# Pool mixer and second norm of a decoder layer: whole float32 products, a small bias, transposes, another opening

## The chip, the cores and the metric

The kernel runs on one core of a Trainium2 chip. The metric is the device time of one execution in microseconds (us). The engines are TensorE (PE in the profile: matrix products into the accumulation memory PSUM), VectorE (DVE), ScalarE (ACT), GpSimd (POOL) and SyncE (SP, which here issues all transfers). Each engine works through its own list of instructions in order; semaphores make one engine wait for another.

## The reference

One layer: a norm, a causal pooling mixer, a residual sum, a second norm, a gated network with a short convolution, a residual sum. `D_MODEL` and `SEQ` are 1024, the hidden width is 2816.

```python
def rms_norm(x, g):
    y = x * lax.rsqrt(jnp.mean(x * x, axis=-1, keepdims=True) + EPS)
    return y * g

def pool_mixer(x, w, b, scale):            # windows 2, 4, 8, 16: one per group of 256 columns
    cs = cumulative sum of x over the sequence
    window_sum = cs[pos + 1] - cs[max(pos + 1 - w_len, 0)]
    d = window_sum / count - x             # per group
    return scale * (einsum('bsgc,gcd->bsgd', d, w) + b)

def conv_ffn(x, w_in, conv_w, conv_b, w_out):
    h = causal_depthwise_conv(x @ w_in, conv_w, conv_b)
    val, gate = jnp.split(h, 2, axis=-1)
    return (jax.nn.silu(gate) * val) @ w_out

x = x + pool_mixer(rms_norm(x, norm_mix_g), ...)
x = x + conv_ffn(rms_norm(x, norm_ffn_g), ...)
```

## The kernel before

**Precision.** TensorE takes two kinds of float32 here. Plain float32 is exact enough as it is. The rounded kind (`fp32r`) runs faster but keeps fewer bits. So the large products are split: `hi` is the operand rounded by ScalarE, `lo` the rest that VectorE subtracts, and a product is the sum of hi x hi, hi x lo and lo x hi: three passes.

**The mixer, per tile of 128 rows** (`j` from 0 to 7):

- `stat(j)` calls `rstd_of` (L127): ScalarE squares the tile and sums (L130), takes a root (L131), and five small VectorE steps (L132 to L137) give the reciprocal root with one correcting step.
- `mixer_norm(j)` (L145) scales a constant band matrix by that number per row: `bandr`. The band holds 1/w inside the window, and 1/w - 1 on the diagonal.
- `mixer_window(j)` (L188): eight plain products (L151) of the tile with the band give window mean minus tile, transposed, in the PSUM tile `psd`. The first 16 positions are mended: by a factor for tile 0 (L196), by `edges` for the others (L198). ScalarE writes `dh` (L199), VectorE the rest `dl` (L200).
- `mixer_out(j)` (L206): 24 products (L214) of the parts with the weights' parts `wph`, `wpl`, and two (L215) that add the bias, into `psy`. VectorE adds the tile (L217), which is stored for the last residual sum (L218); then the second norm's statistics (`st_b`) and a diagonal matrix `diag` of the reciprocal roots (L221).
- `ffn_operand(j)` (L233): eight plain products (L237) of the tile with `diag` turn and norm it at once into `pst`. The gain of the second norm is one number per partition there: seven pieces on ScalarE (L242), the eighth on VectorE (L244), into `n2f`. Then sums and differences (L271) and splits (L259, L260) make the network's operands.

`edge_norm` and `mixer_edges` do the same for the last 16 rows of every tile (`x_edge`), which reach into the next tile. `mixer_weights` scales the pool weights (L178) and splits them (L183, L184). `mixer_bias` forms scale x bias in all 128 partitions, the high part in 64 of them, the low part in the other 64 (L157 to L162), from a broadcast load of 512 KB.

**The network.** Its first product runs as seven products of half blocks per block of hidden columns instead of eight (operands named `B11`, `T1`, `B22`, `T2` and so on; L303). `load_in(n)` loads 1 MB of weights into a `raw` buffer, `prep_in` makes sums and splits. The first operands (`A11`, `A12` of blocks 0 and 1) and three such products are woven into the last rounds of the mixer loop (L389 to L413); everything from L415 is the network proper.

**Buffers and order.** A tile asks for one of `bufs` buffers under a tag and waits until the last reader of the buffer's former tile is done. Three tags matter: `raw` has two buffers of 8 KB per partition (`wp_raw`, `rows_b`, then the network's blocks), `ha` has one (`x_edge`, later the network's `ha`), `ps` has three in PSUM (`psd`, `psy`, `pst`, `ps_edges`). Each engine's list is laid down when the kernel is built, by a planner that follows the program's order where operands are ready; `tc.issue_after(ins)` puts what is written inside behind `ins` in the list of that instruction's engine, without waiting for its end.

Of the kernel before, what the change touches and what calls it, by code (L numbers as in the profile page):

```python
# [7 lines left out]
F32 = mybir.dt.float32  # L8
# [18 lines left out]

CW, CB, GM = 0, 3 * 2 * NF, 4 * 2 * NF
# [5 lines left out]
BD = B0 + NG * P  # L34

NOPS_A = 3
ACT_GAIN = 7
# [6 lines left out]
def trunk_kernel(ctx: ExitStack, tc: tile.TileContext, x, consts, par, rows, pool_w, w_in, w_out, out):  # L44
# [31 lines left out]
    def load_x(j):  # L76
        if j < 2 or j == NS - 1:
            xs[j] = work.tile([P, D], F32, tag="hl", name=f"x{j}", bufs=7)
        else:
            xs[j] = pp.tile([P, D], F32, tag="x", name=f"x{j}", bufs=5)  # L80
        nc.sync.dma_start(xs[j], x[j * P : (j + 1) * P, :])
# [8 lines left out]
    nc.gpsimd.memset(x_edge[:HALO, :], 0.0)  # L90
    for g, w in enumerate(WINDOWS):

        e = edge_band[:, g, :].rearrange("p (j t) -> p j t", t=HALO)
        nc.gpsimd.memset(edge_band[:, g, :], 1.0 / w)
        affine(e, e, ALU.is_gt, 0.0, w - HALO, [[-HALO, NS], [-1, HALO]], 1)
        affine(e, e, ALU.is_ge, 0.0, HALO - 1, [[HALO, NS], [0, HALO]], -1)
    for g, w in enumerate(WINDOWS):

        m = band[:, g, :]
        nc.gpsimd.memset(m, 1.0 / w)  # L100
        affine(m, m, ALU.is_ge, 0.0, 0, [[1, P]], -1)
        affine(m, m, ALU.is_gt, 0.0, w, [[-1, P]], 1)
        affine(m, m, ALU.not_equal, 1.0 / w - 1.0, 0, [[1, P]], -1)
    par_sb = const.tile([P, NPAR], F32, tag="par", name="par_sb")
    wp_raw = raw_tile("wp_raw").rearrange("p a (c d) -> p (a c) d", d=GRP)
    rows_b = raw_tile("rows_b")
    scale_b, bias_b = rows_b[:, 0, :], rows_b[:, 1, :]
    load_x(0)
    nc.sync.dma_start(cst, consts)
    nc.sync.dma_start(x_edge[HALO:, :], x.rearrange("(j r) d -> j r d", r=P)[: NS - 1, P - HALO :, :])  # L110
# [11 lines left out]
    nc.vector.memset(eps_t, EPS)  # L122
    ident = cst[:, :FAC]
    fac = cst[:, FAC:B0].rearrange("p (c t) -> p c t", t=HALO)
    band0 = cst[:, B0:].rearrange("p (g s) -> p g s", s=P)

    def rstd_of(src, name):  # L127
# [3 lines left out]
        nc.scalar.activation(st[:, 1:2], st[:, 0:1], AF.Sqrt, bias=eps_t, scale=1.0 / D)  # L131
        nc.vector.tensor_scalar(st[:, 0:1], st[:, 0:1], 1.0 / D, EPS, op0=ALU.mult, op1=ALU.add)  # L132
        nc.vector.reciprocal(st[:, 2:3], st[:, 1:2])

        nc.vector.scalar_tensor_tensor(st[:, 3:4], st[:, 2:3], st[:, 0:1], st[:, 2:3], op0=ALU.mult, op1=ALU.mult)
        nc.vector.tensor_scalar(st[:, 3:4], st[:, 3:4], -0.5, 1.5, op0=ALU.mult, op1=ALU.add)
        nc.vector.tensor_tensor(st[:, 2:3], st[:, 2:3], st[:, 3:4], ALU.mult)  # L137
        return st[:, 2:3]

    bands, marks, stats = {}, {}, {}  # L140

    def edge_norm():
        nc.vector.tensor_scalar(edge_band, edge_band, rstd_of(x_edge, "e"), None, op0=ALU.mult)

    def mixer_norm(j):  # L145
        t = bands[j] = pp.tile([P, NG, P], F32, tag="bandr", name=f"bandr{j}", bufs=2)
        nc.vector.tensor_scalar(t, band if j else band0, stats[j], None, op0=ALU.mult)

    def windows(ps, src, weights):
        for c in range(NK):  # L150
            nc.tensor.matmul(ps[:, c * P : (c + 1) * P], src[:, c * P : (c + 1) * P], weights[:, c // 2, :], start=True, stop=True)  # L151


    bias_hl = pp.tile([P, D], F32R, tag="bias_hl", name="bias_hl")
    mean_w = pp.tile([P, P], F32R, tag="mean_w", name="mean_w")

    def mixer_bias():  # L157
        nc.vector.memset(mean_w.bitcast(F32), 2.0 / P)
        nc.vector.tensor_tensor(bias_b, bias_b, scale_b, ALU.mult)
# [489 lines left out]
```

## Time and profile before

| | us |
|---|---|
| median of 3 runs (721.27 to 721.67) | 721.29 |
| the profiled execution | 723.45 |
| its span, first to last instruction | 721.7 |
| TensorE busy in the span | 698.9 (97%) |
| VectorE busy | 609.7 (84%) |
| ScalarE busy | 352.3 (49%) |
| the network's products, L303 (1848) and L576 (924), mean ns of one | 390 to 394 |

How to read it: a line of the table by stretch has the length, then for PE, PEld (weight loads), DVE, ACT and POOL the busy time and the number of instructions, then the clock granted to TensorE as a share of full speed, the busy share of the transfer engines, and GB/s. A line of the chain of waits has start, length, engine, tile and line of the work that the end of the span hung on. A line of the groups has line, engine, operation, output and inputs, shapes and count, then busy time and the mean of one in ns, then idle time of the engine ahead of it and what ended that. A matrix product's recorded length overlaps the next one's, so what a row of them costs is told by the distance between starts, or by the chain. One call of a plain float32 product leaves two records.

### The profile page before, as it was taken

To read this page: it belongs to the slowest core of one execution; us is meant where nothing else is said; L and a number is where in the kernel's file an instruction comes from. 1 tells how busy PE (TensorE), PEld (TensorE's weight loads), DVE (VectorE), ACT (ScalarE), POOL (GpSimd) and SP (SyncE) were. 2 spreads that over 40 slices of the span, in tenths; PEclk is the share of its full clock that TensorE was granted. 3 is DMA by queue.
4 is the path that set the end of the run, shared out by engine and by line. 5 is a ranking of instruction groups with operands and counts; after the bars stand their busy time and mean duration, and the time that the engine had idled before them with its cause. 6 is when DMAs were issued, how large, how long until landed. Compare 5 with 4: busy or idle time off the path is not lost.

```text
span 721.7 us, 8803 instructions
## 1 busy us (share of the span) xinstructions
PE 698.9 (97%) x3252; PEld 580.2 (80%) x3252; DVE 609.7 (84%) x941; ACT 352.3 (49%) x566; POOL 7.7 (1%) x33
## 2 busy tenths in 40 slices
PE   3799999999999999999999999999999999999997
PEld 3799977888888888888888888888888788888886
DVE  3788999999888898888888888877996998798994
ACT  4597746554444444444444444444553444344441
POOL 4000000000000000000000000000000000000000
PEclk9899999999999999999999999999999999999999
DMA  9722030222222222222122112227999910005241
GB/s 266 282 89 84 34 117 0 118 88 88 88 87 88 88 88 89 87 88 81 66 89 73 58 75 87 88 89 264 315 321 312 308 54 1 0 1 190 87 152 67
DMA packets 30881, 83.83 MB, mean 116 GB/s; under 512 B 3335, under 2 KB 4487, under 8 KB 28023
## 3 DMA queue, kind: packets, MB, share of 16 engines
q1 hardware_dynamic: 30839, 83.28, 32.8%
q8 instruction: 25, 0.41, 0.2%
q14 instruction: 17, 0.14, 0.1%
HBM read 63.34 MB, written 19.92 MB: 115 GB/s over the span
## 4 chain that ended last, share of the span: by engine, by line
PE 80%; DVE 11%; DMA 6%; issue 1%; SPq 1%; ACT 1%; DVEq 0%; ACTq 0%
PE Y L303 23%; PE oP L576 21%; PE X L303 15%; PE Z L303 15%; PE psy L214 3%; DMA blk<-g_dram 3%; PE psd L151 2%; DMA x<-in_x_dram 1%; PE pst L237 1%; DVE n2f L271 1%; DVE oBP L70 1%; DVE T L260 1%; DMA blk<-in_w_out_dram 1%; DVE blk L271 1%; DVE oAP L70 1%
## 5 line engine op out<-in xcount | busy, mean ns | idle before, releaser
L576 PE MATMUL oP<-oBP,oAP 128*128 128x512 f32 x924 | 210.8, 390 | 1.0 <-ACT oBP L69 0.6
L576 PEld LDWEIGHTS oP<-oBP,oAP 128*128 128x128 f32 x924 | 173.2, 188 | 38.5 <-DVE oBP L70 1.4
L303 PE MATMUL X<-B,A11s 128*128 128x512 f32 x264 | 65.6, 394 | 0.7 <-DVE A11s L70 0.7
L303 PE MATMUL Y<-T,S2s 128*128 128x512 f32 x264 | 65.1, 394 | 1.1 <-DVE T L260 1.0
L303 PE MATMUL Z<-B,S4s 128*128 128x512 f32 x264 | 64.1, 392 | 0.6 <-DVE r L337 0.6
L303 PE MATMUL Z<-T,S1s 128*128 128x512 f32 x264 | 64.6, 393 | 0.0
L303 PE MATMUL Y<-T,S3s 128*128 128x512 f32 x264 | 64.3, 392 | 0.0
L303 PE MATMUL Y<-T,A22s 128*128 128x512 f32 x264 | 64.1, 392 | 0.0
L303 PE MATMUL X<-B,A12s 128*128 128x512 f32 x264 | 63.4, 390 | 0.0
L303 PEld LDWEIGHTS Y<-T,S2s 128*128 128x128 f32 x264 | 49.2, 188 | 13.2 <-DVE T L260 1.5
L303 PEld LDWEIGHTS X<-B,A11s 128*128 128x128 f32 x264 | 49.3, 188 | 12.3 <-DVE A11s L70 1.1
L303 PEld LDWEIGHTS Z<-B,S4s 128*128 128x128 f32 x264 | 49.5, 188 | 11.8 <-issue 1.1
L303 PEld LDWEIGHTS Z<-T,S1s 128*128 128x128 f32 x264 | 49.5, 188 | 11.4 <-ACT S1s L69 0.2
L303 PEld LDWEIGHTS Y<-T,S3s 128*128 128x128 f32 x264 | 49.6, 188 | 11.2
L303 PEld LDWEIGHTS Y<-T,A22s 128*128 128x128 f32 x264 | 49.5, 188 | 11.1 <-ACT val L350 0.3
L303 PEld LDWEIGHTS X<-B,A12s 128*128 128x128 f32 x264 | 49.5, 188 | 10.3
L361 ACT ACTIVATE gate<-gate 128x1024 f32<-128x1024 f32 x22 | 23.4, 1061 | 43.5 <-DVE gate L352 43.5
L69 ACT ACTIVATE oBP<-blk 128x512 fp32r<-128x512 f32 x32 | 20.2, 633 | 46.9 <-PE oP L576 41.6
L351 DVE SCALAR_TENSOR_TENSOR val<-ha,par_sb,val 128x1023 f32<-128x1023 f32 x22 | 28.2, 1282 | 12.5 <-ACT val L350 12.5
L343 DVE TENSOR_TENSOR ha<-Z,q 128x512 f32<-128x512 f32 x20 | 13.8, 691 | 23.9 <-PE Z L303 23.9
L69 ACT ACTIVATE S4s<-win 128x512 fp32r<-128x512 f32 x22 | 13.9, 633 | 40.4 <-PE Z L303 35.9
L350 ACT ACTIVATE gate<-hb,par_sb 128x1024 f32<-128x1024 f32 x22 | 27.4, 1245 | 11.9 <-DVE hb L345 11.9
(130 smaller groups left out, 1094.2 us busy)
## 6 DMA issues: line engine op xcount, KB each, us to landing
win<-in_w_in_dram SPq DMA_DIRECT2D x22, 1024.0 KB, 4.8
g_dram<-val SPq DMA_DIRECT2D x22, 512.0 KB, 2.6
blk<-g_dram SPq DMA_DIRECT2D x33, 256.0 KB, 5.4
blk<-in_w_out_dram SPq DMA_DIRECT2D x31, 256.0 KB, 5.5
A12s<-g_dram SPq DMA_DIRECT2D x22, 256.0 KB, 5.0
B21s<-in_w_out_dram SPq DMA_DIRECT2D x22, 256.0 KB, 3.5
x<-in_x_dram SPq DMA_DIRECT2D x8, 512.0 KB, 10.4
x_dram<-x SPq DMA_DIRECT2D x8, 512.0 KB, 2.6
```

What stands on the lines that cost most here:

```text
L69: nc.scalar.activation(t[:, 0, :], src, AF.Copy)
L70: nc.vector.tensor_tensor(t[:, 1, :], src, t[:, 0, :].bitcast(F32), ALU.subtract)
L151: nc.tensor.matmul(ps[:, c * P : (c + 1) * P], src[:, c * P : (c + 1) * P], weights[:, c // 2, :], start=True, stop=True)
L214: nc.tensor.matmul(o, a[:, c, :], w[:, c, :], start=c % 4 == 0 and i == 0, stop=False, skip_group_check=True)
L237: nc.tensor.matmul(ps[:, c * P : (c + 1) * P], x1[:, c * P : (c + 1) * P], diag, start=True, stop=True)
L271: nc.vector.tensor_tensor(out, a, b, ALU.subtract)
L303: nc.tensor.matmul(bank, a[:, i, ks], b[:, l, k, :], start=opens and m == 0, stop=m == 11, skip_group_check=not opens)
L343: tt(hid[n, "a"][:, NH:], bank, hid[n, "q2"], ALU.add)
L350: nc.scalar.activation(t, src, AF.Identity, bias=par_sb[:, CB + f : CB + f + 1], scale=w[2])
L351: nc.vector.scalar_tensor_tensor(t[:, 1:], src[:, : S - 1], w[1], t[:, 1:], op0=ALU.mult, op1=ALU.add)
L361: nc.scalar.activation(gate, gate, AF.Silu)
L576: nc.tensor.matmul(obanks[set_, i], a[:, u, i * P : (i + 1) * P], b[:, v, :], start=opens and g == 0 and m == 0, stop=g == NP2 - 1 and m = ...
```

## The change

- **Pool's product** takes `dh` and the scaled weights `wp_raw` as plain float32: eight calls of 256 columns instead of 24 of parts. `dl`, `wph`, `wpl` and their splits go. `wp_raw` is so read until the last tile.
- **The bias** is loaded as 8 rows of 128 (`rows8`), multiplied there, split into high and low row, and the two rows are moved by two small transfers into rows 0 and 1 of a tile that GpSimd clears; the product with a matrix of ones adds them.
- **The second norm**: VectorE forms `n2` = tile x reciprocal root x gain in one pass (`ffn_norm`), for which the gain lies in all partitions as `gain_b`. That tile is made in the opening: VectorE spreads the gain over the identity matrix (`spread`), two plain products with the matrix of ones (`gain_rows`) sum it into every partition, ScalarE copies it out, under the tag `ha`. `ffn_operand` turns `n2` by `nc.tensor.transpose`; the splits read PSUM, and ScalarE copies to `n2f` what is needed later in one pass.
- **The norm's small steps** are three instead of five, the correcting step folded into two factors; the constant `FOLD` that this leaves stands in the bands and in the gain.
- **The opening**: other order of loads; edge bands come from the host instead of GpSimd; 12 and 4 idle products (`keep_warm`); a root taken first on ScalarE; a list of `issue_after`. `sums_in` forms the sums of blocks 0 and 1 in the last rounds of the loop.

```diff
+    keep_warm(12)
     load_x(0)
-    nc.sync.dma_start(cst, consts)
-    nc.sync.dma_start(x_edge[HALO:, :], ...)
+    nc.sync.dma_start(cst[:, :E0], consts[:, :E0])
     nc.sync.dma_start(par_sb, par)
+    nc.sync.dma_start(rows8, rows.rearrange("r (k p) -> k r p", p=P))
     nc.sync.dma_start(scale_b, rows[:1, :].to_broadcast([P, D]))
-    load_x(1)
     for g in range(0, NG, 2):
         nc.sync.dma_start(wp_raw[...], pool_w[...])
+    nc.sync.dma_start(x_edge, x.rearrange("(j r) d -> r j d", r=P)[P - HALO :, :, :])
+    nc.sync.dma_start(cst[:, E0:], consts[:, E0:])
+    load_x(1)
     load_x(2)
-    nc.sync.dma_start(bias_b, rows[1:, :].to_broadcast([P, D]))
-    for j in range(3, NS):
-        load_x(j)
...
+    def pool_bias():
+        b8 = rows8[:, 1, :]
+        nc.vector.tensor_tensor(b8, b8, rows8[:, 0, :], ALU.mult)
+        nc.scalar.activation(bias8[:, 0, :], b8, AF.Copy)
+        nc.vector.tensor_tensor(bias8[:, 1, :], b8, bias8[:, 0, :].bitcast(F32), ALU.subtract)
+        for l in range(2):
+            nc.sync.dma_start(bias_hl[l : l + 1, :].bitcast(F32), bias8[:, l, :].bitcast(F32))
+
+    def gain_rows():
+        ps = bank2("ps_gain")
+        flat = spread.rearrange("p k s -> p (k s)")
+        for h in range(2):
+            cols = slice(h * NH, (h + 1) * NH)
+            nc.tensor.matmul(ps[:, cols], ones.bitcast(F32), flat[:, cols], start=True, stop=True)
+        gain_b = work.tile([P, D], F32, tag="ha", name="gain_b", bufs=1)
+        marks["gain"] = nc.scalar.activation(gain_b, ps, AF.Copy, scale=FOLD).ins
+        return gain_b
...
     def mixer_window(j):
         ps = bank2(f"psd{j}")
-        windows(ps, xs[j], bands.pop(j))
-        dh = pp.tile([P, NK, P], F32R, tag="dh", name=f"dh{j}", bufs=2)
-        dl = pp.tile([P, NK, P], F32R, tag="dl", name=f"dl{j}", bufs=1)
+        last = windows(ps, xs[j], bands.pop(j))
+        if j == 0:
+            with tc.issue_after(last):
+                gains.append(gain_rows())
+                keep_warm(4)
+        dh = pp.tile([P, NK, P], F32, tag="dh", name=f"dh{j}", bufs=2)
...
-        nc.scalar.activation(dh, ps3, AF.Copy)
-        nc.vector.tensor_tensor(dl, ps3, dh.bitcast(F32), ALU.subtract)
+        marks[f"dh{j}"] = nc.scalar.activation(dh, ps3, AF.Copy).ins
...
     def mixer_out(j):
+        for c in range(NK):
+            o = ps[:, c // 2 * GRP : (c // 2 + 1) * GRP]
+            nc.tensor.matmul(o, dh[:, c, :], wp_raw[:, c, :], start=c % 4 == 0, stop=False, skip_group_check=True)
         for h in range(2):
-            for c in range(4 * h, 4 * h + 4):
-                for i, (a, w) in enumerate(((dh, wph), (dh, wpl), (dl, wph))):
-                    nc.tensor.matmul(o, a[:, c, :], w[:, c, :], ...)
-            nc.tensor.matmul(ps[:, cols], mean_w, bias_hl[:, cols], ...)
+            m = nc.tensor.matmul(ps[:, cols], ones, bias_hl[:, cols], ...)
...
+    def ffn_norm(j):
+        x1, r = n2s[j]
+        n2 = n2s[j] = pp.tile([P, D], F32, tag="n2", name=f"n2_{j}", bufs=2)
+        nc.vector.tensor_tensor(r[1], r[0], r[1], ALU.mult)
+        nc.vector.scalar_tensor_tensor(n2, x1, r[1], gains[0], op0=ALU.mult, op1=ALU.mult)
...
     def ffn_operand(j):
         for c in range(NK):
-            nc.tensor.matmul(ps[...], x1[...], diag, start=True, stop=True)
+            nc.tensor.transpose(ps[:, c * P : (c + 1) * P], n2[:, c * P : (c + 1) * P], ident)
-        for c in range(ACT_GAIN):
-            nc.scalar.activation(n2f[:, c, cols], ps3[:, c, :], AF.Identity, scale=gain[:, c : c + 1])
-        nc.vector.tensor_tensor(n2f[:, rest, cols], ...)
         if j < NS // 2:
-            split_n(nops["B11"], n2f[:, lo, cols], cols)
-            split_n(nops["B21"], n2f[:, hi, cols], cols)
+            split_n(nops["B11"], ps3[:, lo, :], cols)
+            split_n(nops["B21"], ps3[:, hi, :], cols)
+            nc.scalar.activation(n2f[:, :, cols], ps3, AF.Copy)
             return
...
     stat(0)
-    for j in range(NS + 4):
+    mixer_norm(0)
+    with tc.issue_after(marks["band0"]):
+        gain_spread()
+    with tc.issue_after(marks["spread"]):
+        pool_bias()
+        mixer_window(0)
+    for j in range(3, NS):
+        load_x(j)
+    with tc.issue_after(marks["first"]), tc.issue_after(marks["dh0"]):
+        mixer_weights()
+        edge_norm()
+        with tc.issue_after(marks["gain"]):
+            stat(1)
+        mixer_norm(1)
+    with tc.issue_after(marks["band1"]), tc.issue_after(marks["a1"]):
+        mixer_out(0)
+    with tc.issue_after(marks["psy0"]), tc.issue_after(marks["a1"]):
+        mixer_edges()
+        stat(2)
+    for j in range(2, NS + 4):
         if j < NS:
             mixer_norm(j)
...
         if 0 <= j - 1 < NS:
             mixer_window(j - 1)
...
+        if 1 <= j - 2 < NS:
+            mixer_out(j - 2)
         if 0 <= j - 2 < NS:
-            mixer_out(j - 2)
+            ffn_norm(j - 2)
...
+        if j in (9, 10):
+            with tc.issue_after(marks[2 * j - 13]):
+                sums_in(j - 9)
```

More of the change, by code (lines that the diff above doesn't have):

```diff
@@ L107, in trunk_kernel, with keep_warm @@
-    scale_b, bias_b = rows_b[:, 0, :], rows_b[:, 1, :]
+    rows_raw = raw_tile("rows_raw")
+    scale_b = rows_raw[:, 0, :]
+    rows8, bias8 = (rows_raw[:NK, 1, i * NH : i * NH + 2 * P].rearrange("k (r p) -> k r p", p=P) for i in range(2))
+    bias8 = bias8.bitcast(F32R)
+    idle = work.tile([P, NH], BF16, tag="sum", name="idle", bufs=3)
+    nc.vector.memset(idle, 0.0)
+    idle_ps = bank2("idle_ps")[:, :NH]
+    def keep_warm(n):
+        for _ in range(n):
+            nc.tensor.matmul(idle_ps, idle[:, :P], idle, start=True, stop=True)
@@ L149, in windows @@
     def windows(ps, src, weights):
         for c in range(NK):
[L151 to L159, printed above, removed]
-        nc.scalar.activation(bias_hl, bias_b, AF.Copy)
-        low = slice(P // 2, P)
-        nc.vector.tensor_tensor(bias_hl[low, :], bias_b[low, :], bias_hl[low, :].bitcast(F32), ALU.subtract)
+            m = nc.tensor.matmul(ps[:, c * P : (c + 1) * P], src[:, c * P : (c + 1) * P], weights[:, c // 2, :], start=True, stop=True)
@@ L287, in prep_in @@
             sub(a11, a21, a11)
-        if op == "S4":
+        if op == "S4" and (n, "S4") not in sums:
             sub(a12, a12, a11)
```

132 lines of the change are left out of this document (67 added, 65 removed).

## The prediction, made before the result was known

> **What bounds the kernel now.** I read the page's head, then (next fence) a table of busy time by stretch, cut where the chain of waits changes its engine, then the chain itself.
>
> ```profile
> span 721.7 us, 8803 instructions
> ```
>
> ```profile
> core 0: us, PE busy (x) PEld busy (x) DVE busy (x) ACT busy (x) POOL busy (x), PEclk, DMA share, GB/s
> 8.66:12.06 3.40, 3.40 (x16) 3.21 (x16) 0.00 (x0) 0.66 (x1) 0.00 (x0) 1.00 1.02 226
> ...
> 23.00:25.22 2.22, 0.00 (x0) 0.00 (x0) 2.22 (x6) 1.75 (x3) 0.00 (x0) 0.99 0.45 183
> 25.22:28.15 2.93, 2.93 (x13) 2.93 (x14) 2.21 (x6) 1.02 (x1) 0.00 (x0) 0.50 0.76 281
> ...
> 31.46:75.75 44.29, 44.29 (x356) 43.16 (x357) 36.51 (x106) 35.86 (x88) 0.00 (x0) 1.00 0.22 88
> 75.75:95.00 19.25, 19.25 (x110) 16.80 (x109) 19.25 (x37) 14.55 (x38) 0.00 (x0) 1.00 0.07 29
> 95.00:112.00 17.00, 14.61 (x62) 10.96 (x62) 17.00 (x22) 8.72 (x11) 0.00 (x0) 1.00 0.34 124
> ```
>
> Three stages can be seen. Until 31.46 us TensorE runs in bursts with gaps: this is the opening. From 31.46 to 75.75 TensorE has no gap at all (44.29 of 44.29) while VectorE rests 7.8 us of it. From 75.75 to 112.00 it is VectorE that has no gap (19.25 and 17.00), and TensorE loses only 2.4 us. All that the change touches lies before 112 us; behind it the gated network runs as before, bound by TensorE, so what is won by 112 us should be kept to the end.
>
> The chain of waits gives the rhythm of the middle stage, one tile of 128 rows after another:
>
> ```profile
> 35.07 1.78 PE psd L151 x16
> 36.86 1.43 PE psy L214 x12
> 38.28 0.23 PE psy L215
> ...
> 40.19 1.78 PE pst L237 x16
> ...
> 47.09 1.78 PE pst L237 x16
> ...
> 67.82 1.78 PE pst L237 x16
> ...
> 75.48 0.25 PE psy L215
> ...
> 75.75 1.23 DVE x L217
> ```
>
> Per tile: window sums (psd) 1.78 us, the Pool product with its bias (psy) 3.33 us from 36.86 to 40.19, the turning of the second norm (pst) 1.78 us; a period of 6.90 us (40.19 to 47.09). The last psy ends at 75.73; call that the mixer's end.
>
> **The product in whole float32.** Before, a tile takes 24 products of parts, 0.119 us apart (1.43 us for 12), and two bias products. After, it takes 8 calls of 256 columns in plain float32. The trace has plain float32 only at 128 columns: eight calls leave 16 records (psd, pst), 0.111 us apart. The groups tell how such a record scales:
>
> ```profile
> L214 PE MATMUL psy<-wph,dl 128*128 128x256 f32 x64 | 18.1, 283 | 0.0
> ...
> L215 PE MATMUL psy<-bias_hl,mean_w 128*128 128x512 f32 x16 | 6.7, 421 | 0.0
> ...
> L237 PE MATMUL pst<-diag,x 128*128 128x128 f32 x128 | 15.4, 275 | 0.0
> ```
>
> A plain record of 128 columns lasts 275 ns, almost what a rounded one of 256 columns lasts (283), so it seems to stream each column twice. Then 16 records of 256 columns cost 16 x 0.222 = 3.55 us, with the bias (0.46) 4.01: 0.68 us more per tile. The other end, a record that costs the same at any width (16 x 0.119 = 1.90), would be 0.97 us less per tile; the durations speak against it, and I take the 0.68.
>
> **The turning in transpose mode.** No transpose is in the trace. The nearest row is L237: two records a call, 1.78 us a tile. I expect one record a call at that row's spacing, since 128 weight columns are still loaded for each: 0.89 us, a gain of 0.89 per tile. The ends are 1.78 (two records again) and streaming alone: 256 columns more cost 421 - 283 = 138 ns, so 128 cost 69 ns, and eight 0.55 us. [...] The period becomes 1.78 + 4.01 + 0.89 = 6.68 instead of 6.90.
>
> **What leaves and joins VectorE and ScalarE.**
>
> ```profile
> L242 ACT ACTIVATE n2f<-pst,par_sb 128x128 f32<-128x128 f32 x56 | 16.4, 379 | 4.7 <-PE pst L237 4.7
> ...
> L200 DVE TENSOR_TENSOR dl<-psd,dh 128x1024 fp32r<-128x1024 f32 x8 | 9.7, 1218 | 6.5 <-PE psy L214 6.3
> L217 DVE TENSOR_TENSOR x<-psy,x 128x1024 f32<-128x1024 f32 x8 | 9.7, 1215 | 1.2 <-PE psy L215 1.1
> ...
> L199 ACT ACTIVATE dh<-psd 128x1024 fp32r<-128x1024 f32 x8 | 8.2, 1026 | 1.8 <-DVE psd L198 1.8
> L271 DVE TENSOR_TENSOR n2f<-n2f 128x512 f32<-128x512 f32 x12 | 8.0, 682 | 1.0 <-ACT n2f L242 1.0
> ...
> L244 DVE TENSOR_TENSOR n2f<-pst,par_sb 128x128 f32<-128x128 f32 x8 | 2.3, 286 | 0.1
> L221 DVE TENSOR_SCALAR diag<-cst,st_b 128x128 f32<-128x128 f32 x8 | 2.2, 280 | 0.0
> ```
>
> VectorE loses the low part dl (9.7 us), diag and the eighth gain product (2.2, 2.3) and some small norm steps; it gains the whole normed tile n2, eight passes of 1024 elements like L217 (9.7). ScalarE gives 56 gain copies (16.4) for one or half a pass per tile (1.03 or less, L199). Both had slack in the middle stage, so there this costs and brings nothing: TensorE hides it. If TensorE came under 5.5 us a tile, VectorE would set the pace; 6.68 is clear of that.
>
> **The opening.** The order of loads decides it. Bytes before:
>
> ```profile
> 0.00:5.00 5.00, 0.00 (x0) 0.00 (x0) 0.22 (x2) 2.07 (x2) 4.37 (x19) 1.00 0.64 209
> 5.00:10.00 5.00, 1.34 (x6) 1.34 (x7) 1.47 (x6) 1.94 (x4) 3.32 (x15) 1.00 1.00 179
> 10.00:15.00 5.00, 2.64 (x17) 2.45 (x16) 1.45 (x7) 2.39 (x4) 0.00 (x0) 0.99 1.05 330
> 15.00:20.00 5.00, 3.96 (x24) 3.67 (x23) 4.43 (x13) 4.24 (x9) 0.00 (x0) 0.67 1.04 402
> ```
>
> That is 1.05 MB by 5 us, 1.94 by 10, 3.59 by 15, 5.60 by 20. In the new order the pool weights are complete after 2.47 MB (x0 512 KB, constants 256, parameters 96, rows 8, scale 512, weights 1024), so near 11.6 us; edge rows, edge constants, x1, x2 follow, and behind them in the same queue the two bias rows, after 4.17 MB, near 16.4 us. The idle products warm the clock for psd0 (3.40 us in the first table instead of 1.78), but psd0 then waits for nothing that helps: psy0 needs the scaled weights (eight VectorE passes, row L178 below, the first four while the second half of the weights loads: until about 14) and, for its last two products, the bias rows at 16.4. So psy0 ends near 16.9 and the edge sums (1.78, as psd), which are put behind it, near 18.7. That x0's root needs no table load any more only brings psd0 forward, which is not late. On SP the bias rows wait for their parts; behind them stand the loads of x3 to x7. The transfers ahead fill the wire until 16.4 anyway, so that wait costs nothing unless the rows come later than that. POOL's clearing of the bias tile lies behind a shorter list than before.
>
> Here I see a new wait. The gain copy writes a tile under the tag "ha", which has one buffer, and the edge rows hold it until the edge sums have read them. The statistics of x1 are put behind the gain copy on ScalarE. So the order is edge sums (18.7), gain copy (1.03: 19.7), squares and root of x1, small steps and band, then psd1. These rows price the statistics, the weights' passes and the band:
>
> ```profile
> 14.06 1.06 ACT L130 ACTIVATE junk_a<-x 128x1024 bf16<-128x1024 f32 x1 [1.18 <-DMA x<-in_x_dram]
> ...
> 15.24 0.29 ACT L131 ACTIVATE st_a<-st_a,eps_t 128x1 f32<-128x1 f32 x1
> ...
> 15.71 0.47 DVE L178 SCALAR_TENSOR_TENSOR wp_raw<-rows_b,par_sb,wp_raw 128x256 f32<-128x256 f32 x1
> ...
> 18.28 0.47 DVE L147 TENSOR_SCALAR bandr<-band,st_a 128x512 f32<-128x512 f32 x1
> ```
>
> From 14.06 to 15.53 is 1.5 us (21.2); the band takes 0.47 and the three small steps with their hand-overs, by my estimate, 0.7 (22.4). Queued behind a1 on ScalarE are the edge copy, a2 and the squares of the first sum; TensorE stands empty from 18.7 to 22.4. In the first table an empty 2.22 us (23.00 to 25.22) was followed by a clock of 0.50, so I price psd1 at 3.40: 25.8. [...] Then dh (1.03), behind a fix of the first rows for which I allow 0.3, reaches 27.1, psd2 fills to 27.6, psy1 ends at 31.6. Before, psy1 ended at 35.07. The opening wins 3.5 us.
>
> **The sum.** To psy2: 1.78 + 4.01 = 5.79 for 5.12 (35.07 to 40.19), -0.67. Four periods to psy6: 4 x 0.22 = +0.9. To the mixer's end once more a pst and a psy change: -0.89 + 0.68, 0.2 less. So the mixer's end comes 3.5 - 0.67 + 0.9 + 0.2 = 3.9 us earlier. Behind it VectorE sets the end at 112. It loses three gain products (0.9), one diag (0.3) and four sums of block 0, which may now run in its idle time before (4 x 0.68 = 2.7). It gains n2 of the last tile (1.2) and the two first splits of block 1 (1.4), because block 1 now loads late: wp_raw, until now free after its split, is the operand of the last psy, and both "raw" buffers are needed for the two blocks. Net 1.3 less. Together 5.2 us. The profiled execution took 723.45 us (span 721.7), the median of three runs is 721.29; 5.2 off each gives 718.2 and 716.1. I say 716.1.
>
> **Rivals.** (1) The gain copy isn't held up, or the loads come earlier than the old byte curve says. Then psd1 follows the edge sums at 18.7 (20.5), dh1 is there at 21.8, psd2 ends at 22.3, psy1 at 26.3: the opening wins 8.8, in all 10.5, and the time is 710.8. Against it: the single buffer. For it: everything except x1's place behind the gain copy would be ready.
>
> (2) Block 1 stops the queue; this ends slower. Its load can only start at the mixer's end, and the trace has two rows for what follows:
>
> ```profile
> win<-in_w_in_dram SPq DMA_DIRECT2D x2, 1024.0 KB, 6.1
> ...
> 87.83 0.69 DVE L260 TENSOR_TENSOR T<-n2f,T 128x512 fp32r<-128x512 f32 x1
> ```
>
> The load takes 6.1, its first split about 1.3 (two passes of 512). If that split stands on VectorE ahead of the last tile's sum, the whole run to T1 (87.83 + 0.69, 12.8 us behind the mixer's end) slides by 7.4: 5.2 - 7.4 is 2.2 slower, 723.5. It decides from the point where the planned order has the split in front of L217 of tile 7; behind it the load hides under the waiting TensorE work.
>
> (3) The transpose is no cheaper. Two records a call: five turnings lie before the mixer's end (40.19 to 67.82 in the chain), 5 x 0.89 = 4.5 of the 5.2 go, 720.6. If in addition they did not overlap, 275 ns each as L237 lasts, a tile would pay 2.2 instead of 0.89: 5 x 1.31 = 6.6, and three more of which TensorE's 2.4 us of slack covers most: about 1.5; 2.9 slower, 724.2. [...] The spacing of 0.111 at a duration of 275 in L237 speaks for overlap.
>
> (4) The transpose costs streaming only, 0.55: 5 x 0.34 = 1.7 more, 714.4.
>
> **How the numbers follow.** Forecast 0.44 (with both bounds of the Pool product beside it, 713.5 to 718.5); rival (1) 0.20; (2) 0.12; (3) 0.05 for two records and 0.03 without overlap; (4) 0.16. What a measurement can tell here is 0.2%, 1.4 us. Faster: forecast, (1) and (4), less 0.04 for forecasts that fall short: 0.76. Same: two records and those 0.04: 0.09. Slower: (2) and no overlap: 0.15. The range from 709.0 to 721.2 leaves out (2), the no-overlap case and the best ends of (1).
>
> **What would show it.** Right: psy about 4.0 us and its turning about 0.9 in the chain; an empty TensorE of some 3 us ahead of psd1 that ends on the band, with the gain copy behind the edge sums on ScalarE; psy1 ending near 31.6, the last psy near 71.8. Wrong: psd1 right behind the edge sums (rival 1); a split of block 1 that ends a long wait on a load behind the last psy (rival 2); two turning records a call (rival 3). A psy of 2.4 us would overthrow the double streaming.

## The result and the profile after

The changed kernel takes 728.95 us (median of 4 runs, 727.32 to 729.68); the kernel before, run beside it, 721.28 us (4 runs, 719.23 to 721.67). The ratio is 1.0109, with a 95% interval from 1.0083 to 1.0135. The change makes this kernel about 1.1% slower; I had forecast 0.7% faster. The profiled execution took 729.68 us. The head of its page:

```profile
span 728.0 us, 8475 instructions
```

The span is 6.3 us longer than before's 721.7. The table by stretch, cut again where the chain of waits changes its engine (length, then busy time of PE, PEld, DVE, ACT and POOL, then granted clock, transfer share, GB/s):

```profile
18.20:22.34 4.14, 4.10 (x18) 3.71 (x18) 0.10 (x1) 0.00 (x1) 0.00 (x0) 0.59 1.03 411
22.34:26.12 3.78, 0.00 (x1) 0.04 (x1) 1.19 (x5) 3.26 (x5) 0.00 (x0) 0.88 0.84 344
26.12:32.24 6.12, 3.75 (x17) 3.49 (x17) 4.11 (x11) 4.94 (x11) 0.00 (x0) 0.50 0.23 91
32.24:39.71 7.47, 7.47 (x36) 6.96 (x37) 2.37 (x9) 2.43 (x5) 0.00 (x0) 0.79 0.01 3
39.71:79.33 39.62, 39.62 (x243) 35.81 (x242) 32.45 (x69) 26.69 (x48) 0.00 (x0) 1.00 0.20 80
79.33:118.03 38.70, 33.50 (x146) 26.86 (x144) 36.59 (x53) 21.31 (x33) 0.00 (x0) 0.91 0.26 95
```

The last line begins where the last psy ends (79.33) and ends at the first product X of the next block, which before stood at 112 (111.88). From 22.34 to 32.24 TensorE works 3.75 us out of 9.90; this hole is the new thing. Between 39.71 and 79.33 it has no gap, as before. Behind that VectorE has 2.1 us of gaps, where before it had none.

The chain of waits (start, length, what), from the bias rows on:

```profile
11.84 6.22 DMA bias_hl<-rows_raw
...
18.20 1.03 PE psy L242 x2
19.23 3.08 PE ps_edges L170 x16
22.34 1.02 ACT gain_b L209
23.36 1.04 ACT junk_a L148 x2
...
25.47 0.55 DVE bandr L157
26.01 1.14 DVE x L245
27.18 1.16 ACT junk_b L148 x2
...
29.52 1.28 DVE n L253
30.87 0.22 DVE psd L227
31.11 1.03 ACT dh L228
...
32.24 3.55 PE psd L170 x16
35.79 3.46 PE psy L239 x16
39.24 0.47 PE psy L242 x2
...
45.41 0.87 PE pst L268 x8
...
52.00 0.87 PE pst L268 x8
...
75.39 3.47 PE psy L239 x16
78.87 5.14 DMA win<-in_w_in_dram
84.04 0.64 ACT A11s L74
84.72 6.86 PE X L341 x18
...
118.03 2.56 PE X L341 x10
```

Read from the top, this is the opening that I described, and then more. The bias rows, the edge sums, the gain copy on ScalarE, the squares of x1 and its band follow each other as forecast, up to 26.01. There I had TensorE back at work. The chain instead goes on through tile 0's own sum (L245), its squares (junk_b), its normed tile `n2` (the rows write it "n", L253), and only then to the mending of tile 1's first rows (L227), `dh1` and the sums of tile 2. TensorE takes up its work at 32.24, and psy1 ends at 39.71. Before it ended at 35.07.

The waits of TensorE (who waits, for whom, us in total, times, longest) name the same places:

```profile
PE psd L170 <- ACT edges L180: 3.8, 1, 3.8
PE X L341 <- ACT A11s L74: 3.7, 1, 3.7
PE psd L170 <- ACT dh L228: 2.4, 1, 2.4
PE psy L242 <- DMA bias_hl<-rows_raw: 2.1, 1, 2.1
```

The first is psd1, behind the gain copy and the statistics of x1; the edge copy that the table names follows them on ScalarE and ended at 25.63, x1's band only at 26.01. The second is the late load of block 1.

The difference is made in three places. To the end of psy1: 39.71 for 35.07, +4.6 us. From there to the end of the last psy: 39.62 for 40.66 (75.73 - 35.07), -1.0. From there to the first X: 38.70 for 36.15 (111.88 - 75.73), +2.6. That is 6.2 of the 6.3; behind X both need 610 us.

### The profile page after: what moved, and what is told of

The parts are those of the page before. It is cut to its first block, busy times and chain, and to the rows that moved or that the text cites. A ratio compares the mean times of both kernels' runs of the same rounds, so it can differ in the third digit from the quotient of the medians.

```text
span 728.0 us, 8475 instructions
## 1 busy us (share of the span) xinstructions
PE 706.4 (97%) x3144; PEld 578.6 (79%) x3144; DVE 605.5 (83%) x897; ACT 342.1 (47%) x515; POOL 4.7 (1%) x21
## 4 chain that ended last, share of the span: by engine, by line
PE 80%; DVE 9%; DMA 7%; ACT 2%; issue 1%; SPq 1%; DVEq 0%; ACTq 0%
PE Y L341 22%; PE oP L632 21%; PE X L341 16%; PE Z L341 14%; PE psy L239 3%; DMA blk<-g_dram 3%; PE psd L170 2%; DMA B21s<-in_w_out_dram 2%; DMA wp_raw<-in_pool_w_dram 1%; DVE oBP L75 1%; DVE blk L299 1%; DMA bias_hl<-rows_raw 1%; DVE T L288 1%; DVE oAP L75 1%; PE pst L268 1%
## 5 line engine op out<-in xcount | busy, mean ns | idle before, releaser
L341 PE MATMUL X<-B,A11s 128*128 128x512 f32 x264 | 67.8, 403 | 4.3 <-ACT A11s L74 3.7
L341 PEld LDWEIGHTS X<-B,A11s 128*128 128x128 f32 x264 | 50.8, 194 | 16.7 <-ACT A11s L74 3.9
L341 PEld LDWEIGHTS Z<-T,S1s 128*128 128x128 f32 x264 | 49.5, 188 | 11.4 <-ACT S1s L74 0.2
L74 ACT ACTIVATE oBP<-blk 128x512 fp32r<-128x512 f32 x32 | 20.3, 633 | 46.9 <-PE oP L632 41.6
L75 DVE TENSOR_TENSOR oBP<-blk,oBP 128x512 fp32r<-128x512 f32 x32 | 22.0, 686 | 11.9 <-ACT oBP L74 11.9
```

The source lines that it names most:

```text
L74: nc.scalar.activation(t[:, 0, :], src, AF.Copy)
L75: nc.vector.tensor_tensor(t[:, 1, :], src, t[:, 0, :].bitcast(F32), ALU.subtract)
L341: nc.tensor.matmul(bank, a[:, i, ks], b[:, l, k, :], start=opens and m == 0, stop=m == 11, skip_group_check=not opens)
```

## The experiments

**Theories.** A: the gain copy in the one buffer of `ha` and, behind it, the order of the statistics stretch the opening, and the pool weights kept in a `raw` buffer stretch the part behind the mixer; the new operations themselves cost what they were forecast to. Rival B: TensorE's half clock in the opening (granted 0.59 and 0.50 in the stretches from 18.20 and from 26.12) is the loss, and the waits are hidden beside it. Rival C: the bias rows, which come late through the queue, hold everything. Rival D: one of the new operations (float32 product, turning) loses on its own. The bias in rows, the shorter norm steps and the new order of loads were not taken out singly. All times are medians, each ratio is to the kernel before on the same chip; the three columns on the right are ends of psy1 and of the last psy and the start of X in the profiled run.

| kernel | us (n) | ratio to before, 95% | psy1 ends | last psy ends | X starts |
|---|---|---|---|---|---|
| before | 721.28 (4) | 1 | 35.07 | 75.73 | 111.88 |
| the change | 728.95 (4) | 1.0109, 1.0083 to 1.0135 | 39.71 | 79.33 | 118.03 |
| gain copy in own buffer | 724.18 (7) | 1.0039, 1.0022 to 1.0056 | 35.51 | 75.12 | 113.89 |
| pool weights in own buffer | 726.01 (10) | 1.0050, 1.0034 to 1.0065 | 38.99 | 78.56 | 112.71 |
| both buffers | 721.62 (10) | 0.9996, 0.9978 to 1.0014 | 34.32 | 73.92 | 108.06 |
| the change, kept warm | 729.13 (4) | 1.0101, 1.0075 to 1.0127 | 37.22 | 76.80 | 116.05 |
| both buffers, x2 first | 718.02 (8) | 0.9943, 0.9927 to 0.9959 | 31.75 | 71.32 | 105.47 |
| ... and bias part first | 717.57 (4) | 0.9942, 0.9927 to 0.9957 | 30.23 | 69.82 | 103.97 |
| before, float32 product | 722.95 (10) | 1.0013, 0.9997 to 1.0029 | 32.10 | 76.19 | 112.36 |
| before, new turning | 730.30 (4) | 1.0114, 1.0097 to 1.0131 | 35.42 | 73.49 | 118.48 |
| bias part first, order of ScalarE | 715.12 (4) | 0.9900, 0.9871 to 0.9929 | 30.07 | 69.67 | 103.81 |
| ... and bias rows written ahead | 714.70 (4) | 0.9898, 0.9868 to 0.9928 | 29.40 | 68.96 | 103.11 |
| bias part first, old turning | 721.74 (10) | 0.9991, 0.9973 to 1.0010 | 30.30 | 74.42 | 107.02 |
| bias part first, no idle products | 717.08 (5) | 0.9933, 0.9907 to 0.9960 | 30.91 | 70.46 | 104.62 |

### The gain copy in its own buffer

```diff
-        gain_b = work.tile([P, D], F32, tag="ha", name="gain_b", bufs=1)
+        gain_b = pp.tile([P, D], F32, tag="gain_b", name="gain_b")
```

> The changed kernel with one edit: the gain copy gets a buffer of its own instead of the one that the edge rows hold. Held-buffer theory: in the changed kernel the gain copy starts at 22.34 us, right behind the edge sums, and the statistics of x1 behind it; with its own buffer it follows the gain products near 11.6, x1's statistics follow its landing, psd1 follows the edge sums near 21 to 22 and psy1 ends near 30 instead of 39.7. Time near 720 (718 to 723), from 728.95. Rival, the added work on TensorE (the span has 7.5 us more of it busy than before): no wait that was removed matters, time within 1.5 us of 728.95. Rival, the clock: only the gap ahead of psd1 that let the clock fall to 0.50 matters; taking it away gives the three halved bursts back, at most 5 us, 724.

psy1 ends 4.2 us earlier than in the change, and by the ratios the kernel takes 0.7%, 5 us, less. So the held copy cost over half of the loss, and yet only half of the 8.1 us by which my forecast of the opening failed. The wait for the edge copy is gone from TensorE's waits; a new one stands in its place (waits, then ScalarE's instructions from 22 us on, then VectorE's; start, length, instruction):

```profile
PE psd L170 <- issue: 4.3, 1, 4.3
```

```profile
22.26 1.06 ACT L148 ACTIVATE junk_b<-x 128x1024 bf16<-128x1024 f32 x1 [2.46 <-DVE x L245]
...
24.41 1.04 ACT L148 ACTIVATE junk_a<-x 128x1024 bf16<-128x1024 f32 x1
```

```profile
25.44 1.28 DVE L253 SCALAR_TENSOR_TENSOR n<-x,st_b,gain_b 128x1024 f32<-128x1024 f32 x1
...
27.32 0.55 DVE L157 TENSOR_SCALAR bandr<-band,st_a 128x512 f32<-128x512 f32 x1
```

psd2 starts at 27.96. Its band (27.32) stands behind `n2` of tile 0 on VectorE, and the squares of x2 (24.41) behind those of tile 0's sum (22.26) on ScalarE, which had rested 2.46 us waiting for that sum. The table says "issue" because it doesn't find a releaser; the order experiment below shows that it is this.

### The pool weights in their own buffer

```diff
-    wp_raw = raw_tile("wp_raw").rearrange("p a (c d) -> p (a c) d", d=GRP)
+    wp_raw = pp.tile([P, 2 * NG, GRP], F32, tag="wp", name="wp_raw")
```

> The changed kernel with one edit: the pool weights get a buffer of their own, so that block 1 of the network's weights can load during the mixer, as before the change. Held-buffer theory: in the changed kernel TensorE waits 3.7 us for the first split of block 1 (load issued at 78.87, landed at 84.0), and the stretch from the last psy to the first product of block 2 is 39.2 us, 3.0 longer than before; this goes, with about 1 us more for the splits of block 1 that can move ahead: time 724.5 to 726.5. Added-work rival: within 1.5 us of 728.95. Clock rival: the half clock behind that gap goes too, some 2 us more, 723.

As expected. Block 1 is loaded long before the mixer ends, and the wait for its split is gone. The stretch from the last psy to X:

```profile
78.56:112.71 34.15, 31.59 (x146) 24.82 (x145) 34.06 (x49) 19.25 (x29) 0.00 (x0) 1.00 0.21 77
```

34.15 us instead of 38.70, a gain of 4.55: VectorE has 2.5 us less to do in it (34.06 for 36.59), because splits and sums of block 1 moved into its idle time earlier (ahead of the last psy it works 34.50 of 39.57 us, in the change 32.45 of 39.62), and 2.0 us less idleness (0.1 for 2.1). This profile gives 1.7 of the 5.3 us back behind X; the timed gain over the change, by the ratios, is 0.6%, 4 us.

### Both buffers

> Both buffers of their own. Held-buffer theory: the two waits lie one after the other on the chain, so the gains add: about 9 and 4 us, time near 716 (713 to 719), which is what was forecast for a change without the hold-up minus the mis-sized rest. If the two hide each other (VectorE sets the end behind the mixer anyway), time near 720. Added-work rival: 727 or more.

Missed by over 5 us. The two gains nearly add up (0.70% and 0.59% singly, 1.13% or 8 us together), and the kernel is level with the one before. The profiled execution was the fastest of the ten (719.73), that of the kernel before lies 2 us above its median; so the table shows X 3.8 us earlier where the medians are level. What is missing to 716 stands in its waits, psd2's from the first experiment:

```profile
PE psd L170 <- issue: 4.1, 1, 4.1
```

### The change, with TensorE kept warm

Idle products are put where TensorE waits, 9 ahead of psy0's bias products and 18 behind the edge sums; their PSUM tile comes from another pool.

```diff
-        windows(ps, x_edge, edge_band)
+        with tc.issue_after(windows(ps, x_edge, edge_band)):
+            keep_warm(18)
...
+        if j == 0:
+            with tc.issue_after(m.ins):
+                keep_warm(9)
```

> The changed kernel with idle products in the two gaps of the opening (9 ahead of the first tile's bias products, 18 behind the edge sums), their PSUM tile moved to the other pool; no wait is taken away. Held-buffer theory: the waits stay and only what ran at half clock on the chain gets shorter: edge sums 3.1 to 1.8, psd2 3.55 to 1.8; psd1 is hidden by VectorE's pass for tile 0: 3 us less, near 726. Clock rival: the three bursts at half clock are the loss of the opening: 5 us less, near 724, and psd1 starts no earlier. Added-work rival: more idle products, no gain or a loss.

The edge sums take 1.80 us instead of 3.08, as they do at a granted clock of 1.00 with the pool weights in their own buffer, and psd1 starts 2.6 us earlier (23.48 for 26.12), 0.9 of it because the bias rows came earlier in this run. psy1 ends 2.5 us earlier. But psd2 still waits (TensorE's waits):

```profile
PE psd L170 <- ACT st_a L149: 4.1, 1, 4.1
```

It stands behind tile 0's sum and `n2` as before, starts at 29.63 and then takes 3.14 us, where the psd after it (37.22) takes 1.78. The timed kernel takes as long as the change (1.0101 beside 1.0109, each good to 0.26%, 1.9 us), where I expected 3 us less. On the change's chain the low clock costs, by my estimate, some 3.4 us: 0.3 in the bias products (1.03 us at a granted 0.59, for 0.71 with the pool weights in their own buffer), 1.3 in the edge sums (3.08 at 0.58, for 1.80 here) and 1.8 in psd2 (3.55 at 0.55, for 1.78 in the kernel before). Idle products alone don't mend the queue: rival B isn't the main cause.

### Both buffers, x2 ahead of tile 0's sum

```diff
+            stat(2)
...
-    with tc.issue_after(marks["band1"]), tc.issue_after(marks["a1"]):
+        mixer_norm(2)
+    with tc.issue_after(marks["band2"]), tc.issue_after(marks["a2"]):
         mixer_out(0)
...
-        stat(2)
```

> Both buffers of their own, and one more edit: the statistics of x2 and its band stand ahead of the first tile's sum and second norm on ScalarE and VectorE. Queue theory: with both buffers mended, TensorE still waits 4.1 us ahead of psd2 because x2's statistics stand behind the squares of tile 0's sum on ScalarE and its band behind tile 0's n2 on VectorE, and the product of tile 1 stands behind psd2 on TensorE; with the edit psd2 follows psd1 and psy1 ends near 28.5 instead of 34.3: 5 us less than with both buffers alone, time near 716.5. Rival, bound by VectorE behind the mixer: the wait goes, but the end of the stretch at the first product of block 2 moves less than 1.5 us. Rival, x2 lands too late for it: psd2 waits for its load, less than 1 us gained.

The median is 3.6 us less where I expected 5, and psy1 ends 2.6 us earlier where I expected 5.8; the ratio goes from 0.9996 to 0.9943, the span from 718.0 to 715.9. psd2's wait is gone, X starts 2.6 us earlier, so VectorE behind the mixer doesn't take the gain back, and the opening is now bound thus (chain of waits):

```profile
22.16 1.14 DVE x L245
...
23.32 1.15 ACT junk_b L148 x2
24.47 0.91 ACT edges L180
...
26.61 0.92 ACT dh L228
...
27.57 3.72 PE psy L239 x16
31.29 0.46 PE psy L242 x2
```

psy1 ends at 31.75. ScalarE's list is the chain, from the landing of the edge rows at 15.94 on: the squares of tile 0's sum wait for VectorE's sum, and edge copy, x3's squares and `dh1` queue behind.

### The bias part ahead of the weights' passes

The low half of the bias is formed ahead of the first scaling of the weights on VectorE, so that its transfer is issued earlier.

```diff
-        nc.vector.tensor_tensor(bias8[:, 1, :], b8, bias8[:, 0, :].bitcast(F32), ALU.subtract)
+        marks["bias"] = nc.vector.tensor_tensor(...).ins
...
-    with tc.issue_after(marks["first"]), tc.issue_after(marks["dh0"]):
+    with tc.issue_after(marks["first"]), tc.issue_after(marks["dh0"]), tc.issue_after(marks["bias"]):
```

> The same, and the low part of the bias ahead of the weights' passes on VectorE, so that the two bias transfers are issued near 9 instead of 11.6 us. If the transfers' delay counts from their issue (6.6 us in the kernel with both buffers), the bias products come 2.7 us earlier, and with them the edge sums and all behind: 2 to 3 us less than the run before. Rival, the queue: the two rows lie behind the edge rows, x1 and x2 in the same queue and land when those have, near 18 either way: less than 0.5 us.

The two times are 0.45 us apart, less than their scatter, and TensorE still waits 2.8 us for the rows. In this profile the bias products start 1.6 us earlier (17.67 for 19.23) and psy1 ends 1.5 us earlier; but the edge rows, which the edit doesn't touch, land 1.5 us earlier too (their squares start at 14.44 for 15.96) and head the chain in both, and behind X the profile gives 1.8 us back. So a gain from the earlier rows is not shown.

### Before, with the whole float32 product

The kernel before, with `dh` and the scaled weights in plain float32 (own buffer), and nothing else.

```diff
-                for i, (a, w) in enumerate(((dh, wph), (dh, wpl), (dl, wph))):
-                    nc.tensor.matmul(o, a[:, c, :], w[:, c, :], ...)
+                nc.tensor.matmul(o, dh[:, c, :], wp_raw[:, c, :], ...)
```

> The kernel before with the Pool product alone in whole float32 (no parts of tile and weights; the scaled weights in a buffer of their own, so that no load is held up). Queue theory: TensorE sets the middle, a tile's product takes 3.93 instead of 3.33 us, seven of them behind the opening: 4 us more; without dl and wpl the opening is 1 to 2 us shorter: 2 to 3 us slower than before. Rival, relief of VectorE counts: 2 us faster or more.

The same time as before (the interval holds 1). A tile's product takes 3.92 us (two halves of 1.73 + 0.23) for 3.33, and the middle stretch 44.1 us for 40.7, 3.4 of the 4 that I had priced; but with the splits gone the opening is 3.0 us shorter (psy1 ends at 32.10), where I had allowed 1 to 2.

### Before, with the new turning

The kernel before with `n2` made by VectorE, transposes, and the gain row made in its opening; the product stays in parts.

> The kernel before with the second norm alone in the new way (n2 on VectorE, formed in place of the tile, gain row made in the opening behind the bias, transposes). Queue theory: a turning takes 0.87 instead of 1.78 us, five lie before the mixer's end: 4.5 us less, of which the gain row gives 1 to 2 back in the opening, where VectorE is busy: 2.5 to 3.5 us faster than before. Rival: n2 on VectorE makes it the bound of the middle, no gain or slower.

A clear miss: 1.1% slower where I expected some 0.4% faster. In the opening the gain's row waits for VectorE (first row below), with the window sums of the next tiles behind it on TensorE, but psy1 ends only 0.35 us later than before. The loss comes after that. First the wait, then the stretch of the mixer from psy3's end on:

```profile
PE ps_gain L214 <- DVE spread L209: 8.3, 1, 8.3
```

```profile
45.67:73.49 27.82, 25.29 (x202) 23.71 (x201) 26.75 (x66) 21.21 (x36) 0.00 (x0) 1.00 0.19 77
```

TensorE, which before had no gap here, now rests 2.5 us, and VectorE works 26.75 of 27.82. VectorE still makes `dl` and makes `n2` as well; psd of one tile starts 7.52 us behind that of the tile before (46.98 and 54.50), then 6.9 and 6.7, where the period before was 6.90 and the cheaper turning alone would give 6.0. By the last psy nothing is lost yet (73.49 for 75.73), but the work that VectorE did in its idle time is late, and from there to X it takes 45.0 us instead of 36.15, with VectorE busy 43.5 of them: from psy3's end to X it works 70.3 us of 72.8. So this part alone loses here, because it moves work to an engine that has no room for it while `dl` is there. It is the one place where rival D holds, and the whole change isn't in it, since there `dl` is gone.

### The order of ScalarE's list

On top of the bias part first: the gain copy ahead of the edge squares, the edge copy ahead of tile 0's sum and squares, x3's statistics behind `dh1`.

```diff
-        edge_norm()
...
+            edge_norm()
...
+    with tc.issue_after(marks["band2"]), tc.issue_after(marks["edges"]):
+        mixer_sum(0, psy0)
...
-        with tc.issue_after(marks["edges"]):
+        with tc.issue_after(marks["dh1" if j == 2 else "edges"]):
```

> The kernel of the last but two run (own buffers, x2's statistics and the bias part moved forward), and ScalarE's list in another order: gain copy ahead of the edge rows' squares, edge copy ahead of the first sum's squares, dh of tile 1 ahead of x3's squares. Queue theory: in that kernel the chain of the opening is ScalarE's list (edge squares 14.4, gain copy, x1, x2, first sum, edge copy, x3, dh at 25.1 to 26.0) and the product of tile 1 starts at 26.05; with the list changed dh of tile 1 comes near 23 and all behind it 2.5 to 3.5 us earlier: near 714.5 where that kernel gives 717.6. Rival, the loads: the chain moves back to the landing of x1 or of the bias rows, less than 1 us.

The time is near what I expected, 715.12 us, 1.0% faster than before, but not by the way that I gave. In the profiled run psy1 ends only 0.2 us earlier than without this step, instead of 2.5 to 3.5, with the edge rows landing 2.4 us later (their squares start at 16.80 for 14.44), and behind X the two profiles differ by 2.2 us in the same instructions (the spans are 713.8 and 716.2). So the number came out, perhaps by luck, and the mechanism is not shown.

### The bias rows written ahead

In the program the two bias transfers stand ahead of the loads of the edge rows, x1 and x2. SyncE's list came out otherwise: the planner puts first what is ready. In the profile the edge rows are issued at 4.03, x1 at 5.67, the bias rows at 8.55 and 9.45, and only x2 stands behind them, at 10.15. So what this run tries is x2's load behind the bias rows.

> The same, and the two bias transfers stand ahead of the loads of edge rows, edge constants, x1 and x2 in the issuing queue. Queue theory: the rows land about when the pool weights have, near 12 to 13, so the 2.8 us wait of the bias products goes; but x1 and the edge rows are issued only when the bias parts exist (near 9), which costs nothing as long as the weights are still on the way: 1 to 2 us less than the run before. Rival: edge rows and x1 land later by as much as the issue waits (up to 4 us), the time grows by 1 to 3 us.

714.70 us; the 0.4 us over the last kernel are within the scatter, and the rows don't land near 12 to 13 but at 17.41. What I expected of rows that are issued first stays untested. It is the lowest median, 1.0% faster than before and 2.1% than the change (0.9898 and 1.0109 of the kernel before). The rows of its chain around the edge sums:

```profile
9.45 7.96 DMA bias_hl<-rows_raw
17.55 0.71 PE psy L238 x2
18.25 3.62 PE ps_edges L166 x16
21.87 3.60 PE psd L166 x32
25.47 3.46 PE psy L235 x16
28.93 0.47 PE psy L238 x2
```

No gap is left from 17.55 to the end of psy1, and the bias rows head the chain here; TensorE waits 1.8 us for them. In the change itself rival C, the bias rows as the main cause, has less room than the wait of 2.1 us: the edge sums, which started at 19.23, need the edge band too, and VectorE's instruction for it ended at 18.31 (first two columns: start, length).

```profile
17.76 0.55 DVE L157 TENSOR_SCALAR edge_band<-cst,st_e 128x512 f32<-128x512 bf16 x1
```

So by these waits, with the rows there the edge sums could have started at most 0.9 us earlier.

### The old turning in the mended kernel

> The kernel of own buffers, x2's statistics and the bias part moved forward, with the second norm in the old way (diagonal matrix, plain products, gains on ScalarE and VectorE; no gain row). With the product in whole float32 TensorE sets the middle, and a turning takes 1.78 instead of 0.87 us: five of them ahead of the mixer's end, 4.5 us; without the gain row on ScalarE the opening wins about 1 us: 3 to 4 us slower than that kernel (717.6), near 721. Rival, VectorE or ScalarE set the middle there: no difference or faster.

As expected: slower than the same kernel with the new turning, by 0.5% or 3.5 us if the ratios are compared (0.9991 and 0.9942). psy1 ends at 30.30 and 30.23, the last psy at 74.42 and 69.82, so the cost is the middle's, 4.5 us in five turnings; 1.5 of it comes back by X. Here, with `dl` gone, TensorE sets the pace, and the turning is worth its 0.9 us a tile.

### Without the idle products

> The same kernel of own buffers and moved forward parts, without the 12 and 4 idle products. Queue theory: psd0 runs at half clock (3.4 instead of 2.05 us), but the products behind it wait for the scaled weights anyway: less than 0.7 us. Clock rival: the product of tile 0 and the gain products run at half clock too and the chain starts later by 2 us or more.

No difference (717.08 and 717.57), though psd0 takes 3.78 us instead of 2.05. That this is half clock would be read from the time alone and is not shown: the mean granted clock of this execution is 1.00, and 1.00 stands in the kernel before beside the 3.40 us of the first table, which my prediction put down to the clock.

## Why the prediction failed, step by step

**Right: the new operations.** The transposes in the groups of the changed kernel (busy us, mean ns of one):

```profile
L268 PE MATMUL pst<-cst,n 128*128 128x128 f32 x64 | 8.1, 272 | 0.0
```

Sixteen records of 256 columns take 3.46 us in the chain, with the bias 3.93, forecast 4.01. A turning leaves 64 records for 64 calls, one a call, and takes 0.87 us, forecast 0.89; the period is 6.59 (45.41 to 52.00), forecast 6.68. The middle stretch gains 1.0 us, forecast 0.4. This leaves rivals (3) and (4) out. The record of a transpose lasts 272 ns, about as long as one of the old turning (275 ns, L237 before); what a transpose costs TensorE is the spacing, 0.87 / 8 = 0.109 us. The turning takes about half of the old 1.78 us.

**Right in kind: the held gain copy.** Edge sums, gain copy, x1's statistics, band and a psd1 at half clock (3.75 us of records, granted 0.50) come in the order I gave, 3.7 us later (psd1 starts at 26.12, forecast 22.4): the bias rows landed at 18.06 instead of 16.4, their products took 1.03 and the edge sums 3.08 near half clock (granted 0.59 and 0.58), where I had 0.5 and 1.78. The bytes came as I had them (4.17 MB were moved by 16.6 us), so the place in the queue alone didn't give the landing.

**Failed: the end of the opening,** "dh (1.03), behind a fix of the first rows for which I allow 0.3, reaches 27.1, psd2 fills to 27.6, psy1 ends at 31.6". psy1 ends at 39.71, 8.1 us later. 3.7 of that came before psd1. The rest is that the step looked at what `dh1` and psd2 need, and not at what stands ahead of them on their engines: the mending of tile 1's first rows and x2's band behind tile 0's sum and `n2` on VectorE, x2's squares behind tile 0's squares on ScalarE, and psd2 ahead of psy1 on TensorE. TensorE rests 2.4 us there and runs psd2 near half clock, 3.55 us at a granted 0.55. The runs bear it out: with both buffers in place, moving x2's statistics and band ahead of tile 0's sum alone brings psy1's end from 34.32 to 31.75. So the 31.6 that I gave to a kernel with a held copy is what one reaches that holds no copy and has the other order as well.

**Failed: the stretch behind the mixer,** "Net 1.3 less". It is 2.6 us longer. I had put block 1's late load down as 1.4 us of VectorE's work; with the load early the stretch is 2.0 shorter than before (34.15 for 36.15; without the late load I would have had 2.7), so the lateness costs 4.55. It is the load of rival (2), at part of its price, and the sign that I named for it, a split of block 1 that ends a long wait behind the last psy, is there. That rival's condition, the split ahead of the last tile's sum, isn't met: the sum starts with the psy's end at 79.34 (L245), its squares at 80.70, and VectorE's split at 84.70. But its `n2` (87.19) and all behind it come after, and TensorE has too little left to do: it runs dry for 3.7 us and then goes on at a lower clock (0.61 over the 6.86 us of X behind the gap, 0.91 over the stretch). "Behind it the load hides under the waiting TensorE work" was wrong.

Together: 8.1 in the opening, less 0.6 in the middle, and 3.9 behind it (2.6 + 1.3), 11.4 us; the span was forecast 5.2 shorter and is 6.3 longer.

**Rival (1)** gave 710.8 with psy1 ending at 26.3. The best order ends it at 29.40 and gives 714.7; the edge sums at half clock (3.62 us for 1.78, granted 0.50 from 19 to 21) and the bias rows (their products end at 18.25, not 16.9) lie between. The bounds 713.5 and 718.5 that stand beside the forecast have no working there; no run bears on them.

**Still open:** where the order of ScalarE's list saves its 2.5 us, and why the same instructions behind X take from 609.3 to 612.4 us in the profiles. In that of the bias part first (612.2) TensorE waits 1.6 us at one place for a split on ScalarE (L74); with the new order of ScalarE (610.0) this wait is 0.2. Why the split came late there isn't known.

## What to carry to other kernels

When a change makes a tile earlier or keeps it longer, list who shares its buffer; a tag with one or two buffers can put a copy behind a whole stage, or a load behind the end of a loop. When a wait is taken out of an opening, work out the chain anew from the next instruction at the head of each engine's list, and not from the operands alone: each repair here uncovered the next wait. And a cheaper operation on one engine that adds a pass on another gains only where the first sets the pace: the same turning lost 1.1% in one neighbourhood and won 0.5% in another. And look at the issuing engine's list in the profile after a reorder: what the program writes first need not be issued first.

## What the runs showed of the hardware

The clock of TensorE doesn't go by the length of the gap ahead alone. In the change a wait of 2.1 us ahead of the bias products is followed by edge sums of 3.08 us, and in the fastest kernel one of 1.8 us by 3.62, both near half clock (granted 0.58 over the former, 0.50 from 19 to 21 us in the latter); with the pool weights in their own buffer the same place has a longer wait and edge sums at full clock (granted 1.00 from 19 to 22 us; waits, then chain):

```profile
PE psy L242 <- DMA bias_hl<-rows_raw: 3.1, 1, 3.1
```

```profile
19.06 0.71 PE psy L242 x2
19.76 1.80 PE ps_edges L170 x16
```

In the fastest kernel the bias products right behind the gap still take 0.71 us, as here, and only the edge sums behind them are slow. No run moves a gap alone, so what else decides the clock was not shown; slow edge sums came behind a wait of 1.8 us, and fast ones behind one of 3.1.

The transfer of the second bias row, 4 KB, took 6.22 us from its issue in the change, and 7.96 in the fastest kernel, where it was issued 2.4 us earlier and ahead of x2's load. It landed 0.65 us earlier for that. By these starts x2's load isn't what holds it: with the bias part first the row is issued at about the same time (9.4) with that load ahead of it, and the bias products start at 17.67, against 17.55 with the load behind. What holds it wasn't tried.
